# Feed-forward of an encoder: the first part's convolution, product and down projection moved behind the next parts' up projections

## The chip, the cores and the metric

The kernel runs on one core of a Trainium2 chip, in one launch. The metric is device microseconds of one execution. Five engines of the core work beside each other, each through its own queue in program order: TensorE (PE in the profile) for matrix products, VectorE (DVE), ScalarE (ACT), GpSimd (POOL) and SyncE (SP), which here issues the DMA transfers. An instruction that waits for a semaphore holds up what stands behind it in its own queue, and nothing else.

## The reference, cut to what matters

Two sequences (256 and 512 positions, 1024 wide) go through two layers. Each layer is a mixer (mLSTM, then windowed attention) and a feed-forward with a convolution of three taps along the sequence. The change touches the feed-forward alone:

```python
def conv_ffn(h, w_up, conv_w, conv_b, w_down):
    u = h @ w_up                                   # 1024 -> 2*2816
    u = conv_general_dilated(u, conv_w[:, None, :], padding=((1, 1),), ...) + conv_b
    g, val = u[..., :D_FF], u[..., D_FF:]
    return (silu(g) * val) @ w_down                # 2816 -> 1024
# in trunk, for each of DEPTH = 2 layers:
    x = x + g1 * y                                 # y: the mixer's output
    h = rmsnorm(x, norm_g[l, 1]) * (1 + sc2) + sh2
    x = x + g2 * conv_ffn(h, ...)
```

All of it is float32. A matrix product is made of three products of rounded halves (hi*hi, lo*hi, hi*lo), so each operand is split into a "hi" and a "lo" tile.

## The kernel before, in words

Both sequences lie side by side as 768 columns; channels lie on the 128 partitions. The hidden width 2816 is cut into 11 parts (NPART). A part has two units of up weights (i = 0 gives the gate rows, i = 1 the value rows, 256 channels each) and one unit of down weights. In the order of the code, a part p does this:

- **`up(p)`**: for i = 0 and 1 a `pair` makes the up product of 256 channels for all columns by a Strassen scheme: seven "quarters" (`quarters`, L1139 to L1146) of 12 matmuls each, 128 x 384. For part 0 a hand-ordered `head` does both units. For part 1 the head has done two of the seven quarters ahead ("rest"), so `pair` has five left. The quarters go by names in the code: `fifth()` fills the bank `e` from the weight sum `s1h`/`s1l`; T2 adds to the bank `b`, whose start is copied in by ACT (L1188); a copy of `b` into the bank `d` by ACT (L1199, the "fork") must stand before T3 adds to `d`; B22 finishes `b`; T4 finishes `d`, after ACT has copied `d` out at T3 (L1210). DVE joins `b` and `e` with these copies (L1212, L1213) into the row tile `urow`, and ACT writes the other halves (L1152).
- Each `pair` loads two weight tiles (`raw`, five buffers, SP), POOL makes sums and differences of them in place (L1172, L1175, L1176, L1184), and ACT and DVE split them: ACT casts the hi part (`whi`, `s1h`, L238), DVE subtracts for the lo part (`wlo`, `s1l`, L239).
- **`conv`**: per 128 channels one ACT instruction (L1357) and two on DVE (L1359, L1360), 128 x 772 each. A part has four such channel groups.
- **`silu`** (ACT, L1367) and **`product`**: POOL multiplies (L1372), ACT casts and DVE subtracts into the split tile `g`. silu of a part is handed to the next `pair`, which issues it behind its fork ("behind").
- **`down(p)`**: the down product, 16 tiles of 6 matmuls; DVE adds each tile to the residual (L567).

The order in which the code names the work is: up(p), then down(p-1), so a part's down product covers the time until the next part's pairs. The engines' queues are then set by a scheduler, which moves instructions within this order by its own estimate of times; `head` alone is fixed by hand. `urows` has one row tile for part 0 and one for all others.

For part 0 the convolution stands right behind the head, its gate and product are handed to the first pair of part 1, and down(0) comes behind the second pair of part 1.

Of the kernel before, what the change touches and what calls it, by code (L numbers as in the profile page):

```python
# [11 lines left out]
R = mybir.dt.float32r  # L12
# [3 lines left out]
P = 128  # L16
# [9 lines left out]
H = T // 2  # L26
# [3 lines left out]
TG = T + GAP  # L30
# [48 lines left out]
def col(t):  # L79

    return t + (GAP if t >= 256 else 0)
# [64 lines left out]
class Net:  # L146
# [1195 lines left out]
    def ffn(self, l, xt, pool, last_tile, apply, keep=None):  # L1342
        nc = self.nc
        u0 = U_FFN + l * NPART * 3
        early = self.prepare(u0)
        next(last_tile)

        urows = [self.slab([P, 4, TG]) for _ in range(2)]
        for urow in urows:
            nc.gpsimd.memset(urow[:, :, 256 : 256 + GAP], 0.0)  # L1350

        behind = []

        def conv(u, y, ch):
            cb = self.cst(CB + l * 44 + ch)
            w = lambda tap: self.cst(CW + (l * 44 + ch) * 3 + tap)
            nc.scalar.activation(y, u, AF.Identity, bias=cb, scale=w(1))  # L1357
            stt = nc.vector.scalar_tensor_tensor
            stt(y[:, 1:], u[:, :-1], w(0), y[:, 1:], ALU.mult, ALU.add)  # L1359
            stt(y[:, :-1], u[:, 1:], w(2), y[:, :-1], ALU.mult, ALU.add)  # L1360


        held = []

        def silu(yrow):
            for j in range(2):
                nc.scalar.activation(yrow[:, j], yrow[:, j], AF.Silu)  # L1367

        def product(yrow, g):
            for j in range(2):  # L1370
                y = yrow[:, 2 + j]
                nc.gpsimd.tensor_tensor(y, y, yrow[:, j], ALU.mult)  # L1372
                self.fp_copy_split(g[:, 0, j], g[:, 1, j], y)

        def up(p):
            urow = urows[0] if p == 0 else urows[1]
            fixed = lambda i: self.bank[i][:, :H]
            if p == 0:
                eng = mybir.EngineType
                self.ready(HALVES[0])  # L1380
                with self.tc.manual_schedule(engines={eng.PE, eng.Activation, eng.DVE}):
                    behind[:] = self.head(u0, last_tile, pool, urows, mark, early)
            yrow = self.slab([P, 4, TG])
            g = self.slab([P, 2, 2, TG], R)
            for i in range(2):
                if p:
                    rows = [urow[:, 2 * i + j] for j in range(2)]
                    with ExitStack() as order:
                        for ins in behind[2 * i :] if p == 1 else ():
                            order.enter_context(self.tc.issue_after(ins))  # L1390

                        other = p == i == 1
                        bank = lambda j: self.pa()[:, :H] if j == 1 and other else fixed(j)
                        self.pair(pool, u0 + 3 * p + i, bank, rows, p == 1, held.pop() if held else None)
                for j in range(2):
                    conv(urow[:, 2 * i + j], yrow[:, 2 * i + j], i * FC + 2 * p + j)
                if i == 0:
                    held.append(lambda: silu(yrow))
            if p:
                product(yrow, g)  # L1400
            else:
                gate = held.pop()
                held.append(lambda: (gate(), product(yrow, g)))
            return g

        def mark(t):

            hi, _ = self.quarter(self.B11)
            self.mm(t, hi[0][:, :P], hi[0], True, True)

        def down(p, g):
            ws = (w for _, w in self.halves(u0 + 3 * p + 2))
            chunk = lambda w, i: [t[:, 512 * i : 512 * (i + 1)] for t in w]

            def tile(w, c, rng):
                s0, s1, _ = rng
                o = self.pa()[:, : s1 - s0]
                cs = slice(c % 4 * P, (c % 4 + 1) * P)
                for i in range(2):
                    wh, wl = chunk(w, i)  # L1420
                    gh, gl = (g[:, z, i, col(s0) : col(s0) + s1 - s0] for z in range(2))
                    self.mm(o, wh[:, cs], gh, i == 0, False)
                    self.mm(o, wh[:, cs], gl, False, False)
                    self.mm(o, wl[:, cs], gh, False, i == 1)
                self.resid(xt, o, l, 40, c, rng)

            if p < NPART - 1:
                for h, w in enumerate(ws):
                    for rng in SAMPLE, PROMPT:
                        for c in range(4 * h, 4 * h + 4):  # L1430
                            tile(w, c, rng)
                return
            ws = list(ws)
            for rng in RANGES:
                norm = Norm(self, xt, rng, apply, last=keep is None and rng is RANGES[-1], adds=None if keep is not None else nc.vector)
                for c in range(KC):
                    tile(ws[c // 4], c, rng)
                    norm.square(c)
                    if keep is not None or rng is not RANGES[-1] or c < 3:
                        self.tick(0.65)  # L1440
                if keep is not None:
                    self.save_x(xt, keep, rng)
                self.start(rng, norm.stages())

        prev = None
        for p in range(NPART):
            g = up(p)
            if prev is not None:
                down(*prev)
            prev = (p, g)  # L1450
        down(*prev)


    def run(self):
# [182 lines left out]
```

## Time and profile before

| what | before |
|---|---|
| median of 3 runs | 1856.12 us (1850.48 to 1857.64) |
| the profiled execution | 1854.76 us, span 1852.7 us |
| PE busy | 1797.8 us, 97% of the span |
| DVE busy | 1394.0 us, 75% |
| ACT busy | 896.9 us, 48% |
| POOL busy | 482.4 us, 26% |
| granted PE clock, mean | 0.991 |

The feed-forward of layer 0 fills about 510 to 1045 us of the span, that of layer 1 about 1310 us to the end. The first parts stand at about 550 to 650 us and 1350 to 1450 us. In a timeline row stand the start, the duration, the engine, the line, the operation, the tiles written and read, the size, and in brackets the idle time of the engine before it and who ended it. In a windows row stand the stretch, its length, and for each engine its busy time and number of instructions.

### The profile page before, as it was taken

What the parts mean: (1) busy time and instruction counts of PE and PEld (TensorE: products, weight loads), DVE (VectorE), ACT (ScalarE), POOL (GpSimd) and SP (SyncE); (2) the same over time, 40 slices, a digit from 0 to 9 for tenths busy, and PEclk for the clock granted to TensorE, in tenths of its full rate; (3) what the DMA queues carried; (4) which work ended last, traced back from release to release, by engine and by line L of the source; (5) the groups of instructions that cost most, each with busy time, mean ns of one, the idle gap of its engine ahead of it and who ended that gap; (6) DMA issues with size and microseconds to landing.
All of it is one profiled execution on the core that took longest, in us unless ns stands there. A gap on an engine that the chain in (4) does not pass through costs nothing.

```text
span 1852.7 us, 29043 instructions
## 1 busy us (share of the span) xinstructions
PE 1797.8 (97%) x11270; PEld 1656.8 (89%) x11270; DVE 1394.0 (75%) x2296; ACT 896.9 (48%) x1816; POOL 482.4 (26%) x387
## 2 busy tenths in 40 slices
PE   7999999999999999999999999999999999999997
PEld 4987887888998999999999888889989999999996
DVE  4755676886689777777777768876898777777777
ACT  4444433444456444444444556764564444444443
POOL 1001001031024333333331303330134333333322
PEclk7999999999999999999999999999999999999999
DMA  8343556546312222222222321133122222222212
GB/s 330 116 148 131 171 192 222 164 143 206 102 46 78 71 67 67 68 69 70 66 69 87 103 83 50 48 95 117 58 83 77 69 69 69 69 69 69 69 35 69
DMA packets 64245, 184.48 MB, mean 100 GB/s; under 512 B 6167, under 2 KB 23831, under 8 KB 64108
## 3 DMA queue, kind: packets, MB, share of 16 engines
q1 hardware_dynamic: 64108, 182.63, 30.4%
q8 instruction: 88, 1.44, 0.3%
q14 instruction: 49, 0.40, 0.1%
HBM read 176.17 MB, written 6.43 MB: 99 GB/s over the span
## 4 chain that ended last, share of the span: by engine, by line
PE 84%; DVE 5%; issue 4%; DMA 3%; ACT 2%; POOL 1%; SPq 0%; POOLq 0%; ACTq 0%; DVEq 0%
PE ps L232 25%; PE pa L232 25%; PE ps L1139 10%; PE ps L1142 10%; PE ps L1140 10%; PE pa L978 1%; DMA raw<-in_adaln_w_dram 1%; DVE wlo L239 1%; DMA raw<-in_w_dram 1%; DVE slab L567 1%; DMA slab<-in_adaln_w_dram 0%; PE pa L1142 0%; PE pa L1140 0%; PE pa L1139 0%; ACT whi L238 0%
## 5 line engine op out<-in xcount | busy, mean ns | idle before, releaser
L238 ACT CAST whi<-raw 128x1024 fp32r<-128x1024 f32 x237 | 248.1, 1049 | 349.1 <-PE pa L232 162.3
L239 DVE TENSOR_TENSOR wlo<-raw,whi 128x1024 fp32r<-128x1024 f32 x237 | 319.6, 1349 | 112.8 <-ACT whi L238 110.9
L232 PE MATMUL pa<-slab,whi 128*128 128x256 f32 (+1 forms) x1472 | 347.4, 332 | 2.8 <-DVE slab L567 2.8
L232 PEld LDWEIGHTS pa<-slab,whi 128*128 128x128 f32 x1472 | 253.9, 189 | 27.1 <-DVE slab L567 4.1
L567 DVE SCALAR_TENSOR_TENSOR slab<-pa,mod,slab 128x256 f32<-128x256 f32 (+1 forms) x368 | 211.3, 592 | 72.0 <-PE pa L232 71.6
L232 PE MATMUL pa<-slab,wlo 128*128 128x256 f32 (+1 forms) x736 | 234.4, 330 | 0.0
L232 PE MATMUL ps<-zh,whi 128*128 128x256 f32 (+1 forms) x560 | 189.3, 339 | 3.7 <-ACT whi L238 1.7
L232 PE MATMUL ps<-zh,wlo 128*128 128x256 f32 (+1 forms) x560 | 184.1, 330 | 2.2 <-DVE wlo L239 2.2
L232 PE MATMUL ps<-zl,whi 128*128 128x256 f32 (+1 forms) x560 | 185.2, 332 | 0.7 <-DVE zl L530 0.7
L1139 PE MATMUL ps<-zh,whi 128*128 128x384 f32 x504 | 172.2, 342 | 3.7 <-ACT nt L1210 1.9
L1140 PE MATMUL ps<-zl,whi 128*128 128x384 f32 x504 | 169.9, 337 | 0.8 <-DVE zl L1096 0.8
L1142 PE MATMUL ps<-zh,wlo 128*128 128x384 f32 x504 | 168.9, 335 | 0.0
L232 PEld LDWEIGHTS pa<-slab,wlo 128*128 128x128 f32 x736 | 139.3, 189 | 13.1 <-DVE wlo L239 0.4
L1175 POOL TENSOR_TENSOR raw<-raw,raw 128x512 f32<-128x512 f32 x40 | 52.2, 1305 | 330.7 <-DVE wlo L239 246.3
L232 PE MATMUL ps<-slab,whi 128*128 128x384 f32 x512 | 132.2, 339 | 2.2 <-ACT sg L819 1.3
L1372 POOL TENSOR_TENSOR slab<-slab 128x772 f32<-128x772 f32 x44 | 86.5, 1968 | 167.6 <-DVE slab L1360 155.7
L1359 DVE SCALAR_TENSOR_TENSOR slab<-slab,cstt,slab 128x771 f32<-128x771 f32 x88 | 104.7, 1192 | 26.6 <-ACT slab L1357 26.4
L232 PEld LDWEIGHTS ps<-zh,whi 128*128 128x128 f32 x560 | 107.4, 192 | 17.5 <-issue 4.4
L484 DVE SCALAR_TENSOR_TENSOR ada<-raw,silc,ada 128x1024 f32<-128x1024 f32 x84 | 110.2, 1349 | 15.1 <-DMA raw<-in_adaln_w_dram 14.9
L232 PEld LDWEIGHTS ps<-zl,whi 128*128 128x128 f32 x560 | 107.4, 192 | 13.0 <-issue 3.4
L232 PEld LDWEIGHTS ps<-zh,wlo 128*128 128x128 f32 x560 | 107.3, 192 | 12.5 <-DVE wlo L239 3.1
L1172 POOL TENSOR_TENSOR raw<-raw 128x512 f32<-128x512 f32 x40 | 64.3, 1608 | 200.2 <-DMA raw<-in_w_dram 161.3
(292 smaller groups left out, 4294.3 us busy)
## 6 DMA issues: line engine op xcount, KB each, us to landing
raw<-in_w_dram SPq DMA_DIRECT2D x208, 512.0 KB, 3.8
raw<-in_adaln_w_dram SPq DMA_DIRECT2D x84, 512.0 KB, 4.6
slab<-in_x_dram SPq DMA_DIRECT2D x12, 512.0 KB, 7.0
slab<-in_adaln_w_dram SPq DMA_DIRECT2D x12, 512.0 KB, 10.3
slab<-mrows SPq DMA_DIRECT2D x8, 384.0 KB, 5.7
xs<-slab SPq DMA_DIRECT2D x6, 512.0 KB, 3.9
bt<-brow SPq DMA_DIRECT2D x16, 192.0 KB, 3.0
slab<-xs SPq DMA_DIRECT2D x6, 512.0 KB, 6.4
```

The lines of the kernel that those rows point to most:

```text
L232: self.nc.tensor.matmul(out, lhsT, rhs, start=start, stop=stop)
L238: nc.scalar.copy(hi, src)
L239: return nc.vector.tensor_tensor(lo, src, hi.bitcast(F32), ALU.subtract)
L484: stt(acc[:, s], row, w, acc[:, s], ALU.mult, ALU.add)
L567: self.nc.vector.scalar_tensor_tensor(x, o, self.mod[l][:, gc + c, q : q + 1], x, ALU.mult, ALU.add)
L1139: mm(o, wh[:, k], hi[k], start=start and k == 0, stop=False, skip_group_check=True)
L1140: mm(o, wh[:, k], lo[k], start=False, stop=False, skip_group_check=True)
L1142: mm(o, wl[:, k], hi[k], start=False, stop=k == 3, skip_group_check=True)
L1172: tt(q[2], q[2], q[3], ALU.add)
L1175: tt(q[0], q[2], q[0], ALU.subtract)
L1359: stt(y[:, 1:], u[:, :-1], w(0), y[:, 1:], ALU.mult, ALU.add)
L1372: nc.gpsimd.tensor_tensor(y, y, yrow[:, j], ALU.mult)
```

## The change

For part 0, `up` now returns after the head. Its convolution, gate and product are issued by the new function `gated` behind the second pair of part 1 (with their own tiles `yrow` and `g`, taken later), ahead of the convolution of that second pair's rows. down(0) moves behind the two pairs of part 2 and stands right ahead of part 2's product and down(1). From part 3 on the order is as before. No instruction is added or taken away on any engine.

```diff
         def up(p):
...
-            yrow = self.slab([P, 4, TG])
-            g = self.slab([P, 2, 2, TG], R)
+            if p == 0:
+                return
             for i in range(2):
...
+                    self.pair(pool, u0 + 3 * p + i, bank, rows, p == 1, held.pop() if held else None)
+                if p == i == 1:
+
+                    gs.append(product(gated(urows[0], 0, (0, 1))))
+                if i == 0:
+                    yrow = self.slab([P, 4, TG])
+                gated(urow, p, (i,), yrow)
+            return yrow
+
+        def gated(urow, p, sides, yrow=None):
+            yrow = self.slab([P, 4, TG]) if yrow is None else yrow
+            for i in sides:
                 for j in range(2):
                     conv(urow[:, 2 * i + j], yrow[:, 2 * i + j], i * FC + 2 * p + j)
-                if i == 0:
+                if i == 0 and p:
                     held.append(lambda: silu(yrow))
-            if p:
-                product(yrow, g)
-            else:
-                gate = held.pop()
-                held.append(lambda: (gate(), product(yrow, g)))
-            return g
+                elif i == 0:
+                    silu(yrow)
+            return yrow
...
+        gs = []
         for p in range(NPART):
-            g = up(p)
-            if prev is not None:
-                down(*prev)
-            prev = (p, g)
-        down(*prev)
+            yrow = up(p)
+            if p == 2:
+
+                down(0, gs[0])
+            if p:
+                gs.append(product(yrow))
+            if p > 1:
+                down(p - 1, gs[p - 1])
+        down(p, gs[p])
```

What the scheduler makes of it stands in the queues. Behind the second T2 quarter of part 1 (it reads `whi_772` before and `whi_769` after, and writes bank `ps_640`), PE's queue before holds the whole fifth quarter of part 2's first pair and then down(0):

```order
L1142 MATMUL ps_640_4535<-zh_94,wlo_773_5696 128x384
L1139 MATMUL ps_639_4534<-zh_94,s1h_807_5941 128x384
L1140 MATMUL ps_639_4534<-zl_95,s1h_807_5941 128x384
L1142 MATMUL ps_639_4534<-zh_94,s1l_808_5942 128x384
L1139 MATMUL ps_639_4534<-zh_94,s1h_807_5941 128x384
```

After, at the same place:

```order
L1142 MATMUL ps_640_4535<-zh_94,wlo_770_5673 128x384
L1139 MATMUL ps_639_4534<-zh_94,s1h_783_5799 128x384
L1140 MATMUL ps_639_4534<-zl_95,s1h_783_5799 128x384
L1139 MATMUL ps_638_4533<-yh_4540,whi_781_5793 128x384
L1140 MATMUL ps_638_4533<-yl_4541,whi_781_5793 128x384
L1139 MATMUL ps_641_4536<-zh_94,whi_771_5676 128x384
```

So only four matmuls of part 2 stand between T2 and T3 (bank `ps_641`, the second pair of part 1), where before there were a quarter and 12 matmuls of down(0).

ACT's queue from the start copy of that pair's bank `b` (L1188) to its fork (L1199), before:

```order
L1188 COPY ps_640_4535<-slab_713_5137 128x384
L238 CAST s1h_807_5941<-raw_803_5930 128x512
L1193 COPY nt_777_5705<-pa_776_5703 128x384
L1357 ACTIVATE slab_756_5577<-slab_713_5137,cstt_75 128x772
L238 CAST whi_780_5790<-raw_779_5788 128x1024
L1152 COPY slab_713_5137<-ps_641_4536 128x128
L1152 COPY slab_713_5137<-ps_641_4536 128x256
L238 CAST slab_755_5564<-slab_754_5563 128x772
L1357 ACTIVATE slab_756_5577<-slab_713_5137,cstt_75 128x772
L1199 COPY ps_641_4536<-ps_640_4535 128x384
```

and after (`slab_712` holds part 0's rows, `slab_713` part 1's, `slab_776` part 0's `yrow`, `slab_764` part 1's):

```order
L1357 ACTIVATE slab_764_5653<-slab_713_5137,cstt_75 128x772
L1188 COPY ps_640_4535<-slab_713_5137 128x384
L1357 ACTIVATE slab_776_5753<-slab_712_5136,cstt_75 128x772 x4
L238 CAST s1h_783_5799<-raw_779_5788 128x512
L1193 COPY nt_774_5682<-pa_773_5680 128x384
L238 CAST whi_781_5793<-raw_780_5790 128x1024
L1152 COPY slab_713_5137<-ps_641_4536 128x128
L1152 COPY slab_713_5137<-ps_641_4536 128x256
L1367 ACT_TABLE_LOAD
L1367 ACTIVATE slab_776_5753<-slab_776_5753 128x772
L1357 ACTIVATE slab_764_5653<-slab_713_5137,cstt_75 128x772
L1199 COPY ps_641_4536<-ps_640_4535 128x384
```

All four convolution instructions of part 0, the table load and a silu now stand ahead of the fork.

POOL's queue at the same place, before:

```order
L1184 TENSOR_TENSOR raw_768_5683<-raw_768_5683,raw_769_5685 128x512
L1172 TENSOR_TENSOR raw_803_5930<-raw_803_5930 128x512
L1372 TENSOR_TENSOR slab_754_5563<-slab_754_5563 128x772
L1172 TENSOR_TENSOR raw_815_6056<-raw_815_6056 128x512
L1175 TENSOR_TENSOR raw_804_5932<-raw_803_5930,raw_804_5932 128x512
```

and after:

```order
L1184 TENSOR_TENSOR raw_765_5660<-raw_765_5660,raw_766_5662 128x512
L1373 TENSOR_TENSOR slab_776_5753<-slab_776_5753 128x772
L1175 TENSOR_TENSOR raw_780_5790<-raw_779_5788,raw_780_5790 128x512
L1373 TENSOR_TENSOR slab_776_5753<-slab_776_5753 128x772
L1176 TENSOR_TENSOR raw_780_5790<-raw_780_5790 128x512
L1184 TENSOR_TENSOR raw_779_5788<-raw_779_5788,raw_780_5790 128x512
```

The two products of part 0 (L1373, the former L1372) now alternate with the weight sums of part 2's first pair (`raw_779`, `raw_780`). In SP's queue the two loads of down(0)'s weights stand behind the four loads of part 2's pairs instead of ahead of them. From part 4 on all queues are the same in both kernels, but for numbers.

More of the change, by code (lines that the diff above doesn't have):

```diff
@@ L1367, in silu, with product @@
                 nc.scalar.activation(yrow[:, j], yrow[:, j], AF.Silu)
-        def product(yrow, g):
+        def product(yrow):
+            g = self.slab([P, 2, 2, TG], R)
             for j in range(2):
@@ L1373, in product @@
                 self.fp_copy_split(g[:, 0, j], g[:, 1, j], y)
+            return g
         def up(p):
@@ L1382, in up @@
                     behind[:] = self.head(u0, last_tile, pool, urows, mark, early)
-            yrow = self.slab([P, 4, TG])
-            g = self.slab([P, 2, 2, TG], R)
+            if p == 0:
+                return
             for i in range(2):
-                if p:
[L1387 to L1394, printed above, removed]
+                rows = [urow[:, 2 * i + j] for j in range(2)]
+                with ExitStack() as order:
+                    for ins in behind[2 * i :] if p == 1 else ():
+                        order.enter_context(self.tc.issue_after(ins))
+                    other = p == i == 1
+                    bank = lambda j: self.pa()[:, :H] if j == 1 and other else fixed(j)
+                    self.pair(pool, u0 + 3 * p + i, bank, rows, p == 1, held.pop() if held else None)
[8 more added lines that the diff above has]
+            for i in sides:
                 for j in range(2):
                     conv(urow[:, 2 * i + j], yrow[:, 2 * i + j], i * FC + 2 * p + j)
-                if i == 0:
+                if i == 0 and p:
                     held.append(lambda: silu(yrow))
-            if p:
-                product(yrow, g)
-            else:
-                gate = held.pop()
-                held.append(lambda: (gate(), product(yrow, g)))
-            return g
+                elif i == 0:
+                    silu(yrow)
+            return yrow
         def mark(t):
@@ L1443, in down @@
                 self.start(rng, norm.stages())
-        prev = None
+        gs = []
         for p in range(NPART):
-            g = up(p)
-            if prev is not None:
-                down(*prev)
-            prev = (p, g)
-        down(*prev)
+            yrow = up(p)
[6 more added lines that the diff above has]
+        down(p, gs[p])
     def run(self):
```

## The prediction

> **What bounds the kernel now.** I read the page first: busy times, then the chain that ended last.
>
> ```profile
> span 1852.7 us, 29043 instructions
> PE 1797.8 (97%) x11270; PEld 1656.8 (89%) x11270; DVE 1394.0 (75%) x2296; ACT 896.9 (48%) x1816; POOL 482.4 (26%) x387
> PE 84%; DVE 5%; issue 4%; DMA 3%; ACT 2%; POOL 1%; SPq 0%; POOLq 0%; ACTq 0%; DVEq 0%
> ```
>
> PE carries the end. So I asked the windows where PE is not full inside the feed-forwards: the middle parts, and the first parts of layer 0 and of layer 1.
>
> ```profile
> 700.00:1000.00 300.00, 300.00 (x1706) 285.16 (x1706) 227.75 (x256) 142.11 (x225) 104.81 (x63) 1.00 0.23 71
> 560.00:580.00 20.00, 17.01 (x91) 15.48 (x90) 19.96 (x17) 13.94 (x22) 10.43 (x5) 1.00 0.26 82
> 1360.00:1380.00 20.00, 16.98 (x91) 15.38 (x90) 19.96 (x17) 13.95 (x22) 10.25 (x5) 1.00 0.27 82
> ```
>
> The middle parts have no idle PE at all, and there the queues of both kernels agree. At the first parts PE idles 3.0 us per layer while DVE (third pair of numbers) is full: 19.96 of 20. Both layers look alike, so I work out one and double it. The waits there, by the view of waits for 555 to 580 us, and how PE's rows start around them:
>
> ```profile
> PE ps L1142 <- DVE s1l L239: 1.4, 1, 1.4
> PE ps L1139 <- ACT nt L1210: 0.9, 1, 0.9
> PE ps L1139 <- ACT ps L1188: 0.7, 1, 0.7
> ...
> 567.22 0.34 PE L1142 MATMUL pa<-zh,s1l 128*128 128x384 f32 x1
> 568.49 0.44 PE L1139 MATMUL ps<-zh,whi 128*128 128x384 f32 x1 [0.93 <-ACT nt L1210]
> ...
> 570.17 0.33 PE L1139 MATMUL ps<-zh,whi 128*128 128x384 f32 x1
> 570.52 0.34 PE L1142 MATMUL ps<-zh,wlo 128*128 128x384 f32 x1
> 571.55 0.44 PE L1139 MATMUL ps<-zh,whi 128*128 128x384 f32 x1 [0.70 <-ACT ps L1188]
> ...
> 573.94 0.34 PE L1140 MATMUL ps<-zl,s1h 128*128 128x384 f32 x1
> 575.64 0.45 PE L1142 MATMUL ps<-zh,s1l 128*128 128x384 f32 x1 [1.36 <-DVE s1l L239]
> ```
>
> Undisturbed, matmuls start 0.174 us apart (570.17 to 570.52 is two). The three waits cost start to start 1.27, 1.03 and 1.70 less 0.174 each, with some 0.1 us lost in the restart rows counted in neither: 3.5 us, and I take **3.8 us** with these restarts. That is all the change can win here.
>
> **The change, part by part.** No instruction is added or removed; all is order. Four moves have one answer together: down(0)'s 96 matmuls and 16 residual adds, its two weight loads on SP, part 0's eight convolution instructions on DVE and four on ACT, and its product. As work they cost the same later. The loads are hidden: DMA's share at this place is 0.26 (the last column but one in the windows). What counts is what they covered. Before, down(0) gave PE work while DVE, ACT and POOL made part 2's weights. After, PE runs the pairs of parts 1 and 2 without it, while part 0's convolution still stands in the same stretch.
>
> I count time from t = 0, the end of the B22 quarter of part 1's first pair, since the first convolution of part 1 waits for it. First PE's side, by its queue after: 10 matmuls of the fifth quarter, 12 of T4, 12 of T2 and the four of part 2, then T3 of the second pair: 38 x 0.174 = 6.6 us.
>
> *The fork (L1199) behind ACT's queue.* The lengths, as starts of neighbours that did not wait:
>
> ```profile
> 558.40 1.05 ACT L1357 ACTIVATE slab<-slab,cstt 128x772 f32<-128x772 f32 x1
> 559.34 0.50 ACT L1199 COPY ps<-ps 128x384 f32<-128x384 f32 x1
> 559.85 1.28 ACT L1367 ACT_TABLE_LOAD   x1
> 561.15 0.85 ACT L1367 ACTIVATE slab<-slab 128x772 f32<-128x772 f32 x1
> 561.90 1.04 ACT L238 CAST whi<-raw 128x1024 fp32r<-128x1024 f32 x1
> 562.84 0.53 ACT L1152 COPY slab<-pa 128x128 f32<-128x128 f32 x2
> ...
> 571.02 0.48 ACT L1188 COPY ps<-slab 128x384 f32<-128x384 f32 x1 [2.58 <-DVE slab L1212]
> 571.44 0.62 ACT L238 CAST s1h<-raw 128x512 fp32r<-128x512 f32 x1
> 571.96 0.47 ACT L1193 COPY nt<-pa 128x384 f32<-128x384 f32 x1
> ```
>
> So: convolution 0.94, fork 0.50, table load 1.30, silu 0.75, cast of a weight tile 0.94, two copies out 0.45, start copy 0.42, small cast 0.52, copy of e 0.42. In the queue after, ahead of the fork: a weight cast that waits for a buffer which B22 reads (done at 1.15), then convolution, start copy, four convolutions, small cast, copy of e, cast, copies out, table load, silu, convolution: 0.94 + 0.42 + 3.76 + 0.52 + 0.42 + 0.94 + 0.45 + 1.30 + 0.75 + 0.94 = 10.4. The fork ends at 1.15 + 10.4 + 0.5 = 12.1, PE came at 6.6: a new wait of **5.5 us**. Behind it on PE stands everything of part 2. Two small casts of part 2 that PE meets on the way are inside this time. The first pair's own fork has only three matmuls (0.52) of cover for its 0.50 and the run-out of T2 (0.34): **0.4 us**.
>
> On the table load the Trainium skill (ScalarE: Activation LUTs, "What ACT_TABLE_LOAD costs") says that a switch costs 1.28 us and another 1.38 us of drain. Here the load takes the same 1.28, but the silu starts 0.02 us after it and the load 0.01 us after the fork, so no drain shows. By that page of the Trainium skill the wait would be 6.9 us and the sum some 2.8 us higher over both layers.
>
> *The next start copy (L1188, part 2's first pair) behind DVE.* DVE's lengths, and what POOL does to them:
>
> ```profile
> 560.11 1.21 DVE L239 TENSOR_TENSOR wlo<-raw,whi 128x1024 fp32r<-128x1024 f32 x1
> 561.25 0.68 DVE L239 TENSOR_TENSOR s1l<-raw,s1h 128x512 fp32r<-128x512 f32 x1
> 561.85 1.01 DVE L1359 SCALAR_TENSOR_TENSOR slab<-slab,cstt,slab 128x771 f32<-128x771 f32 x1
> 562.89 2.51 DVE L1360 SCALAR_TENSOR_TENSOR slab<-slab,cstt,slab 128x771 f32<-128x771 f32 x1
> 565.32 2.31 DVE L239 TENSOR_TENSOR wlo<-raw,whi 128x1024 fp32r<-128x1024 f32 x1
> ...
> 578.67 1.01 DVE L1360 SCALAR_TENSOR_TENSOR slab<-slab,cstt,slab 128x771 f32<-128x771 f32 x1
> 579.61 0.95 DVE L239 TENSOR_TENSOR slab<-slab,slab 128x772 fp32r<-128x772 f32 x1
> 580.48 1.01 DVE L1359 SCALAR_TENSOR_TENSOR slab<-slab,cstt,slab 128x771 f32<-128x771 f32 x1
> ...
> 584.37 0.56 DVE L1213 TENSOR_TENSOR slab<-pa,nt 128x384 f32<-128x384 f32 x1 [1.34 <-ACT nt L1210]
> 584.84 0.55 DVE L1212 TENSOR_TENSOR slab<-ps,nt 128x384 f32<-128x384 f32 x1
> ```
>
> ```profile
> 562.08 2.51 POOL L1372 TENSOR_TENSOR slab<-slab 128x772 f32<-128x772 f32 x1 [5.97 <-ACT slab L1367]
> 564.54 2.01 POOL L1184 TENSOR_TENSOR raw<-raw,raw 128x512 f32<-128x512 f32 x1
> 573.19 1.84 POOL L1372 TENSOR_TENSOR slab<-slab 128x772 f32<-128x772 f32 x1 [4.43 <-DVE slab L1360]
> 590.69 1.29 POOL L1175 TENSOR_TENSOR raw<-raw,raw 128x512 f32<-128x512 f32 x1 [13.02 <-issue]
> ```
>
> Beside POOL, instructions on both sides stretch: L1360 2.51 instead of 1.01, a weight lo 2.31 instead of 1.21, a product 2.51 instead of 1.84. How much of POOL's time lands on DVE, I take from the stretch in which DVE never waits:
>
> ```profile
> 553.15:582.90 29.75, 26.76 (x146) 25.14 (x145) 29.71 (x27) 20.28 (x33) 12.62 (x6) 1.00 0.32 105
> ```
>
> Its DVE instructions, at 1.14 (weight lo), 0.60 (s1l), 0.94 (convolution), 0.87 (product lo), 0.47 (joins), are 5, 4, 12, 2 and 3: 22.5 us. POOL's six, undisturbed, 4 x 1.29 + 2 x 1.84 = 8.8. So 7.2 us of 8.8, or 0.8, land on DVE.
>
> After, DVE's queue from the first weight lo behind t = 1.2 to the join L1212 of part 1's second pair holds 12 convolutions, 2 weight lo, 1 s1l, 2 product lo and 2 joins: 16.8 us. POOL stands beside it with two products and three weight sums: 7.5 us, of which 6.0. So the join ends at 24.0; behind it ACT does convolution, cast, copies and start copy (2.9): T2 of part 2's first pair can start at 26.9. PE comes with 94 matmuls (16.3) and the 5.5: 21.8. Second wait **5.1 us**, between 0 (POOL takes nothing) and 6.6 (all of 7.5).
>
> For the upper end there is a rule: the Trainium skill (SBUF — State Buffer, "SBUF: two separate sides") calls the port pair of VectorE and GpSimd an exclusive lock held for a whole instruction. The stretched rows agree; by it, with nothing hidden, the sum would be 3 us higher over both layers.
>
> *T2 of part 2's second pair*: the same queues go on with 12.5 us of DVE and 6.0 from POOL, to 42.5; PE, 84 matmuls and two of slack behind 26.9, comes at 41.8: **0.7 us** (0 to 2.3). Then down(0) and down(1) follow each other, 33 us of PE, in which DVE catches up; at nothing, by the stretch 700 to 1000 us above, in which six down products run and PE never idles.
>
> Sum per layer: 0.4 + 5.5 + 5.1 + 0.7 - 3.8 = 7.9; both layers 15.8. The profiled execution took 1854.8 (2.1 around its span; 1.4 under the median of 1856.1), so 1870.6; I say **1871 us**.
>
> **The rivals.** (1) *The convolution fits after all.* The three waits go, no others come: 1854.8 - 7.6 = 1847. For it: POOL's weight sums and DVE's order are what held PE before, and both are relieved for part 1. Against: ACT's queue to the fork needs 10.4 us whatever DVE does. It decides for itself where ACT reaches the fork by 6.6. (2) *Only the fork waits*: POOL costs DVE little, since its work falls into DVE's idle time; 2 x (5.9 - 3.8) = 4 more, 1859, no change that shows. Against: the products start only when the convolution ends, so POOL runs where DVE is fullest. (3) *down(0) and down(1) in a row stall too*, as four `pa` banks wait for DVE adds between weight lo tiles of part 3; two weight lo and a blocked one (1.14 + 2.31) late per down, some 3 us per layer: 1877.
>
> **How the numbers follow.** My forecast 0.60 (1864 to 1875), rival 2 0.22, rival 1 0.08, rival 3 0.10. About 0.5%, 9.3 us, is what a measurement of this kernel can tell from no change: slower means above 1865.4, faster below 1846.8. Rival 2 and nearly all of rival 1 lie within; faster is left with 0.03, since 7.6 us is under the bound; same 0.27, slower 0.70. The range runs from rival 2's low side to all upper ends (0.4 + 5.5 + 6.6 + 2.3 - 3.8 = 11.0, twice, 1877) and rival 3: 1857 to 1880.
>
> **What would show it.** Right: the old waits (1.4, 0.9, 0.7) are gone; about 5 us of PE wait for ACT L1199 once per layer, behind the four L1357 and the table load; a wait for ACT L1188 or for a lo tile some 10 us of PE work later; no idle in the middle parts; 560:600 with some 10 us less PE busy than its length. Wrong: L1199 in time (then ACT's order on the chip lets it through sooner), or DVE rows beside POOL unstretched, or idle in the two down products.

## The result: slower by 1%, 1872 us

The changed kernel takes 1872.24 us (median of 5 runs, 1870.58 to 1874.99), the kernel before 1855.68 us (median of 5). The ratio is 1.0096, with a 95% interval of 1.0082 to 1.011: slower by 16 us. The prediction said 1871, within 1857 to 1880.

The page of the changed kernel first: the span, and busy time by engine.

```profile
span 1873.0 us, 29085 instructions
PE 1806.5 (96%) x11270; PEld 1663.9 (89%) x11270; DVE 1397.5 (75%) x2296; ACT 897.5 (48%) x1816; POOL 480.2 (26%) x387
```

DVE, ACT and POOL do what they did before, within 4 us; the 42 instructions that the span line has more than before are waits for semaphores. PE has 9 us more busy time with the same 11270 matmuls, which is the first sign of something that the prediction left out: matmuls that take longer. Outside the two first parts, matmul starts lie as far apart as before, to 1.6 us at any place and to about 1 us in all. The new time stands in 540 to 700 us and 1340 to 1500 us. The profiled run is the slowest of the five (1874.99 us), so its trace shows some 20 us of new time where the medians show 16.6.

PE's waits there, layer 0 of the changed kernel (us in total, how many, the longest):

```profile
PE ps L1139 <- ACT ps L1188: 3.5, 1, 3.5
PE ps L1139 <- ACT ps L1199: 3.3, 1, 3.3
PE ps L1139 <- ACT whi L238: 0.7, 1, 0.7
PE ps L1139 <- ACT s1h L238: 0.7, 1, 0.7
```

The old three (s1l 1.4, L1210 0.9, L1188 0.7) are gone. In their place stand the fork L1199, with two small casts of part 2 just ahead of it, and the start copy L1188 of part 2's first pair. Layer 1 looks alike (3.3 and 2.4). This is ACT's queue up to the fork, in the timeline of the changed kernel:

```profile
566.20 1.05 ACT L238 CAST whi<-raw 128x1024 fp32r<-128x1024 f32 x1 [1.52 <-PE ps L1140]
567.15 1.03 ACT L1357 ACTIVATE slab<-slab,cstt 128x772 f32<-128x772 f32 x1
568.09 0.47 ACT L1188 COPY ps<-slab 128x384 f32<-128x384 f32 x1
568.50 3.81 ACT L1357 ACTIVATE slab<-slab,cstt 128x772 f32<-128x772 f32 x4
...
574.57 1.28 ACT L1367 ACT_TABLE_LOAD   x1
575.87 0.85 ACT L1367 ACTIVATE slab<-slab 128x772 f32<-128x772 f32 x1
576.62 1.02 ACT L1357 ACTIVATE slab<-slab,cstt 128x772 f32<-128x772 f32 x1
577.54 0.47 ACT L1199 COPY ps<-ps 128x384 f32<-128x384 f32 x1
...
592.54 0.49 ACT L1188 COPY ps<-ps 128x384 f32<-128x384 f32 x1
```

t = 0 of the prediction, the end of the quarter that releases the first of these rows, is 566.1 here. The fork ends at 578.0, 11.9 behind it (12.1 was forecast); the start copy ends at 593.0, 26.9 behind it (26.9 was forecast). So both walks through the queues held. What PE does behind each wait shows the part that was not foreseen (timeline of PE; not every matmul is shown):

```profile
578.06 0.69 PE L1139 MATMUL ps<-zh,whi 128*128 128x384 f32 x1 [3.26 <-ACT ps L1199]
...
579.19 0.52 PE L1139 MATMUL ps<-zh,whi 128*128 128x384 f32 x1
...
580.15 0.52 PE L1139 MATMUL ps<-zh,whi 128*128 128x384 f32 x1
...
581.78 0.34 PE L1139 MATMUL ps<-bq,whi 128*128 128x384 f32 x1
...
593.08 0.69 PE L1139 MATMUL ps<-zh,whi 128*128 128x384 f32 x1 [3.46 <-ACT ps L1188]
...
597.09 0.52 PE L1139 MATMUL ps<-yh,whi 128*128 128x384 f32 x1
```

From 579.19 to 580.15 there are three matmuls: 0.32 us each instead of 0.174. The quarter from 578.06 to 581.78 takes 3.72 us instead of 2.09. The windows of the changed kernel give the granted clock (third figure from the end):

```profile
572.00:578.00 6.00, 1.44 (x6) 0.60 (x4) 6.00 (x8) 5.97 (x11) 0.20 (x1) 1.00 0.00 1
578.00:589.00 11.00, 10.94 (x54) 10.94 (x55) 11.00 (x7) 4.72 (x8) 10.93 (x5) 0.84 0.00 1
589.00:593.00 4.00, 0.62 (x4) 0.30 (x2) 3.96 (x5) 3.40 (x7) 0.00 (x0) 0.83 0.10 14
593.00:597.00 4.00, 3.92 (x12) 3.92 (x13) 4.00 (x4) 2.62 (x5) 2.66 (x1) 0.50 0.71 217
597.00:600.00 3.00, 3.00 (x14) 3.00 (x14) 2.45 (x4) 0.70 (x3) 1.28 (x1) 0.75 0.12 46
```

Behind each wait of over 3 us PE runs at half its clock for a while. The Trainium skill (TensorE: Matmul & The Clock Gate, "What's actually happening") says that the clock falls to half after at least one idle window of about 3.4 us, and is whole again after a busy one of about 3.4 us. The trace agrees on the half and on the way back (0.50 behind both waits, 1.00 again 3 to 7 us later). It shows that less idle time is enough: around the second wait the clock falls at 591.7 us, 2.0 us after the last matmul and while PE still waits, which is why the row from 589 us has 0.83. In the kernel before, whose longest wait here is 1.4 us, the granted clock in this place is 1.00.

### The profile page after: what moved, and what is told of

The parts are those of the page before. It is cut to its first block, busy times and chain, and to the rows that moved or that the text cites. A ratio compares the mean times of both kernels' runs of the same rounds, so it can differ in the third digit from the quotient of the medians.

```text
span 1873.0 us, 29085 instructions
## 1 busy us (share of the span) xinstructions
PE 1806.5 (96%) x11270; PEld 1663.9 (89%) x11270; DVE 1397.5 (75%) x2296; ACT 897.5 (48%) x1816; POOL 480.2 (26%) x387
## 4 chain that ended last, share of the span: by engine, by line
PE 83%; DVE 7%; DMA 4%; ACT 3%; issue 2%; POOL 1%; SPq 0%; POOLq 0%; ACTq 0%; DVEq 0%
PE ps L232 26%; PE pa L232 24%; PE ps L1139 10%; PE ps L1140 10%; PE ps L1142 10%; DMA raw<-in_adaln_w_dram 1%; PE pa L978 1%; DVE wlo L239 1%; DMA slab<-in_adaln_w_dram 1%; DVE slab L567 1%; DVE slab L1360 1%; ACT whi L238 1%; DMA raw<-in_w_dram 1%; DVE slab L239 1%; PE pa L1139 1%
## 5 line engine op out<-in xcount | busy, mean ns | idle before, releaser
L567 DVE SCALAR_TENSOR_TENSOR slab<-pa,mod,slab 128x256 f32<-128x256 f32 (+1 forms) x368 | 212.4, 593 | 77.5 <-PE pa L232 77.1
L1373 POOL TENSOR_TENSOR slab<-slab 128x772 f32<-128x772 f32 x44 | 87.7, 1992 | 189.7 <-DVE slab L1360 163.6
L232 PEld LDWEIGHTS ps<-zh,whi 128*128 128x128 f32 x560 | 107.0, 191 | 17.2 <-issue 4.4
L1139 PEld LDWEIGHTS ps<-zh,whi 128*128 128x128 f32 x504 | 96.4, 191 | 21.2 <-ACT ps L1199 10.7
```

The costliest lines, as they stand in the source:

```text
L232: self.nc.tensor.matmul(out, lhsT, rhs, start=start, stop=stop)
L567: self.nc.vector.scalar_tensor_tensor(x, o, self.mod[l][:, gc + c, q : q + 1], x, ALU.mult, ALU.add)
L1139: mm(o, wh[:, k], hi[k], start=start and k == 0, stop=False, skip_group_check=True)
```

## The experiments

The first question was which of the two moves costs the time, and whether ACT's queue, DVE, or the half clock is what holds PE. All ratios are against the kernel before, with 95% intervals.

**1. Only down(0) late.** The order of before, with one move:

```diff
             g = up(p)
-            if prev is not None:
+            if p == 2:
+                down(*first)
+            if prev is not None and p != 1:
                 down(*prev)
+            if p == 0:
+                first = (p, g)
             prev = (p, g)
```

> The kernel before with one edit: down(0) comes behind part 2's pairs, ahead of down(1); the convolution, gate and product of part 0 stay right behind the head, as before. Theory A (the new waits come from part 0's convolution and product standing in the stretch where ACT and DVE are full, not from down(0) itself): the three old waits stay, the fork L1199 of part 1's second pair is in time, and DVE, which was free of part 0's work at 583 us before, joins part 1's second pair in time for the next start copy: 1851 to 1859 us. Rival B (what costs is that PE lost down(0) as cover between the pairs): nearly all of the 16 us is here too, 1866 to 1873 us, with a wait for L1188 or a lo tile at part 2's first pair.

Measured: 1868.48 us, 1.0076 (1.0063 to 1.0088). Theory A fell; rival B holds. The waits of PE, layer 0:

```profile
PE ps L1139 <- ACT nt L1210: 4.8, 2, 2.6
PE ps L1142 <- DVE s1l L239: 1.4, 1, 1.4
PE ps L1142 <- DVE wlo L239: 1.3, 1, 1.3
PE ps L1139 <- ACT ps L1188: 0.7, 2, 0.4
```

The fork is in time, as I had said, but L1210 and a lo tile are late instead. My error was to read "DVE is free at 583" from a trace in which down(0)'s 16.7 us of PE work follow there. Without them PE asks for part 2's tiles at once.

**2. Only the convolution and product late.** The changed kernel with `if p == 1` in place of `if p == 2` ahead of `down(0, gs[0])`.

> The changed kernel with one edit: down(0) comes right behind part 1's second pair again, as before; the convolution, gate and product of part 0 stay behind part 1's second pair. Theory A: the fork's wait for ACT stays (5.4 us per layer by the trace of the changed kernel) and the half clock after it; the second wait turns into one of PE for the product of part 0 on DVE, some 3 us: per layer -3.8 + 0.4 + 5.5 + 2 + 3, about 7, so 1866 us, 1860 to 1872. Rival B (down(0) is the cover that matters): with down(0) back, little is lost, 1852 to 1859 us.

Measured: 1869.42 us, 1.0075 (1.0061 to 1.0088), as theory A had it. The wait for L1199 is 5.3 us, and down(0) then waits 1.9 us (`pa`, L567). So each move alone costs some 14 us, and both together 17. They are not two costs that add up, but two ways to overdraw the same stretch.

**3. The fork ahead of part 0's ACT work.**

```diff
-                    gs.append(product(gated(urows[0], 0, (0, 1))))
+                    with self.tc.issue_after(self.fork_ins):
+                        gs.append(product(gated(urows[0], 0, (0, 1))))
```

> The changed kernel with one edit: the ACT instructions of part 0's convolution, gate and product are held behind the fork L1199 of part 1's second pair. Theory A: the fork stands at 6.3 us from t = 0 instead of 12.1, so the wait for L1199 goes and so does the half clock after it. On DVE ten convolution instructions instead of twelve stand ahead of the join of part 1's second pair, and only weight sums of POOL beside them: join at 18, so no wait for L1188 at part 2's first pair, and the rest of DVE's work falls before part 2's second pair, where some 4 us of wait appear (DVE at 41, PE at 37). Per layer -3.8 + 0.4 + 4: 1856 us, 1851 to 1864. Rival C (DVE and POOL are the bound of the whole stretch, ACT's order only decides where PE waits): the same 10 us come later, 1868 to 1873.

Measured: 1872.57 us, 1.0099 (1.0085 to 1.0113): no gain at all. PE's waits, layer 0:

```profile
PE ps L1139 <- ACT ps L1188: 4.9, 2, 3.0
PE ps L1142 <- DVE wlo L239: 1.5, 1, 1.5
PE ps L1139 <- ACT nt L1211: 1.1, 1, 1.1
```

The 5.4 us at the fork are gone (it ends at 572.5, and PE does not wait for it), and nearly the same time comes back at the next four waits (L1188 twice). This is rival C. The intervals of this run and of the changed kernel overlap, so a gain of two or three us could hide in them; one of 5 us per layer could not.

**4. Work for PE inside the waits.** Behind T2 of part 1's second pair, and ahead of T2 of part 2's first:

```diff
+            with self.tc.issue_after(self.last.ins):
+                for k in range(16):
+                    self.mm(t, hi[0][:, :P], hi[0], k == 0, k == 15)
```

> The changed kernel with 16 further matmuls of 128x384 (2.8 us) per place, whose result nobody reads, behind T2 of part 1's second pair and ahead of T2 of part 2's first pair, where PE waits for L1199 and L1188. Theory D (the waits of over 3 us make the granted clock fall to half for 3.4 to 6.8 us, and that is a loss of its own, some 4 us per layer): the added matmuls lie inside the waits, the clock stays at 1.00, PE comes earlier to the second wait, and what is left is the half-rate time behind the second wait, 2 to 2.5 us per layer: 1867 us, 1864 to 1870. Rival E (the half clock is only in the records, or hidden by the next wait): 1871 to 1878 us, as what is not hidden of the added 2 x 2.8 us per layer is added.

Measured: 1872.06 us, 1.0093 (1.008 to 1.0107). The time is rival E's, at its lower end, but the clock did as theory D said (windows of this kernel, to set beside those of the changed one):

```profile
572.00:578.00 6.00, 6.00 (x36) 6.00 (x36) 6.00 (x7) 5.94 (x10) 0.66 (x1) 1.00 0.00 1
578.00:589.00 11.00, 11.00 (x64) 10.75 (x62) 11.00 (x9) 5.88 (x9) 10.05 (x5) 1.00 0.01 2
593.00:597.00 4.00, 1.19 (x7) 0.87 (x5) 3.97 (x3) 0.95 (x3) 3.15 (x1) 1.00 0.47 135
```

It is 1.00 to 597 us, PE is full to 589 us, and 11.1 us of added matmuls (64 x 0.174) over both layers cost no time. But nothing is won either: PE now waits 3.3 us at the next fork instead (593 to 597; the forks have the line L1203 here):

```profile
PE ps L1139 <- ACT ps L1203: 3.7, 2, 3.3
```

So the half clock behind the first two waits is not what costs the 16 us: it mostly fills time in which PE would wait anyway. That it costs nothing at all is not shown. Behind the last wait the clock falls here too (for 3.4 us from 598.4), and by matmul starts this kernel's first parts, the added matmuls included, are 1.3 and 1.8 us shorter in the two layers than in the trace of the changed one, while the medians (1872.06 and 1872.24) show no gain. In all three rows DVE (third pair) is full. So the next theory was that DVE's work is the bound.

**5. Without DVE's taps for part 0.**

```diff
+            if ch % FC < 2:
+                return
             stt = nc.vector.scalar_tensor_tensor
```

> The changed kernel, with the eight tap instructions (L1359, L1360) of part 0's convolution on DVE left out in each layer; all else stays, ACT's four L1357 and its table load too. Theory F (new, from the four runs before: DVE is full from 567 to 601 us and its total work there is the bound; which engine's order holds PE only decides where PE waits): 7.5 us of DVE per layer fall out, and with them nearly all of the new waits, 7 to 9.7 us per layer: 1856 us, 1852 to 1859. Rival G (ACT's queue ahead of the fork is a cost of its own): the wait for L1199 stays at 5 us with its half clock, the one for L1188 goes: 1865 us, 1862 to 1868.

Measured: 1867.75 us, 1.0068 (1.0052 to 1.0085). Theory F in this plain form fell, and G's number was met without G's mechanism. 15 us of DVE work over both layers were taken away and 5 us came back. PE's waits, layer 0:

```profile
PE ps L1142 <- DVE wlo L239: 2.6, 2, 1.4
PE ps L1139 <- ACT ps L1188: 1.6, 1, 1.6
```

The two waits of 0.7 us for ACT's casts stay as well. The products now come sooner and POOL's work falls in one piece on a DVE that prepares part 2: the lo tile takes 2.02 us instead of 1.21, the tap behind it 2.43 instead of 1.01 (timeline of DVE):

```profile
575.43 2.02 DVE L239 TENSOR_TENSOR wlo<-raw,whi 128x1024 fp32r<-128x1024 f32 x1 [2.78 <-ACT whi L238]
577.54 2.43 DVE L1361 SCALAR_TENSOR_TENSOR slab<-slab,cstt,slab 128x771 f32<-128x771 f32 x1
```

DVE is no longer full here: it idles 2.78 us ahead of this lo tile, and 2.34 us a little earlier, until ACT's casts come, and these stand behind part 0's four L1357 in ACT's queue, the later one behind a table load and a silu too.

**6. POOL's work of parts 0 to 2 on DVE, in the changed kernel.** `nc.vector` in place of `nc.gpsimd` for the sums in `pair` and for `product`, while p < 3.

> The changed kernel, with POOL's weight sums (L1172 to L1184) and products of parts 0 to 2 given to DVE. In the stretch 567 to 601 us of the changed kernel POOL has 15 us of work, about 7 sums and 3 products. Theory F with the price of the prediction (0.8 of POOL's time lands on DVE): DVE is rid of 11.6 us and gets 7 sums at 0.6 and 3 products at 0.87, 6.8 us, so 4.8 us per layer are won: 1862 us, 1858 to 1866. Rival H (POOL's work costs DVE nothing): DVE has 6.8 us per layer more, 1886 us, 1880 to 1890.

Measured: 1868.74 us, 1.0067 (1.0055 to 1.008). Rival H is refuted: DVE has more to do in this stretch and still holds PE up less, by 2.7 us per layer. How that can be stands in the groups of instructions on DVE, 567 to 601 us. The changed kernel (count, busy us, mean ns):

```profile
L1360 DVE SCALAR_TENSOR_TENSOR slab<-slab,cstt,slab 128x771 f32<-128x771 f32 x8 | 10.8, 1345 | 0.1
L1359 DVE SCALAR_TENSOR_TENSOR slab<-slab,cstt,slab 128x771 f32<-128x771 f32 x8 | 10.6, 1344 | 0.0
L239 DVE TENSOR_TENSOR slab<-slab,slab 128x772 fp32r<-128x772 f32 x3 | 5.2, 1720 | 0.0
```

With POOL's work on DVE (567 to 600 us):

```profile
L1360 DVE SCALAR_TENSOR_TENSOR slab<-slab,cstt,slab 128x771 f32<-128x771 f32 x8 | 8.2, 1019 | 0.0
L1359 DVE SCALAR_TENSOR_TENSOR slab<-slab,cstt,slab 128x771 f32<-128x771 f32 x8 | 8.0, 1021 | 0.3 <-ACT slab L1357 0.2
L1373 DVE TENSOR_TENSOR slab<-slab 128x772 f32<-128x772 f32 x4 | 3.8, 956 | 0.0
L239 DVE TENSOR_TENSOR slab<-slab,slab 128x772 fp32r<-128x772 f32 x3 | 2.9, 960 | 0.0
```

The same 19 instructions take 26.6 us beside POOL and 19.1 without it: 7.5 us of stretch, for four products and three sums that POOL does in 11.2 us when alone (4 x 1.84 + 3 x 1.29). That is 0.67 of POOL's time; the prediction had taken 0.8. The Trainium skill (SBUF — State Buffer, "SBUF: two separate sides") has a lock on a shared port pair, held for a whole instruction, and these rows agree with it for the taps and the splits. On DVE itself the seven cost 3.8 + 3 x 0.69 = 5.9, so 1.6 us per layer would be won by this price, an estimate from these rows; 2.7 were measured, and the rest is not accounted for. (In the second window DVE does six sums, since the next pair's three come sooner.) The expected gain of 4.8 us per layer was too large because it took POOL's stretched 15 us, and seven sums instead of three, as its undisturbed work.

**7. The same edit in the kernel before.**

> The kernel before with the same edit: POOL's weight sums and products of parts 0 to 2 are given to DVE. In its full stretch, 553 to 583 us, POOL has four sums and two products, 8.8 us. Theory F: DVE is rid of 7.0 us and gets 4.1, so 2.9 of the 3.8 us of old waits per layer go: 1849 us, 1846 to 1853; this would be faster than both kernels. Rival H: 4.1 us per layer more on a full DVE, 1863 us, 1859 to 1867.

Measured: 1859.83 us, 1.0019 (1.001 to 1.0029). Theory F's 1849 was missed. The reason is another place:

```profile
PE ps L1140 <- DVE zl L1096: 1.9, 2, 1.7
PE ps L1139 <- ACT nt L1210: 1.8, 1, 1.8
```

Part 1's first sums now stand in DVE's queue ahead of the tiles of the input (L1096), for which PE waits at once.

**8 and 9. Without any of part 0's row work, after and before.** In `up`, `gated` and `product` are not called for part 0 (in the kernel before: `for j in range(2) if p else ()`), and down(0) reads the tiles `zh` and `zl`.

> The changed kernel with all of part 0's row work left out in each layer: convolution, gate, product (ACT, DVE and POOL); down(0) multiplies the layer's input tiles instead of the product. Theory I (part 0's row work, put into this stretch, is too much for ACT, DVE and POOL together; the late down(0) is harmless in itself): no PE wait of over 1 us is left at the pairs of parts 1 and 2, the old three waits are gone too: 1850 us, 1846 to 1854. Rival J (without down(0) between them the pairs of parts 1 and 2 alone starve PE, whatever part 0 does): 3 to 6 us of waits per layer stay, 1856 to 1864 us.

> The kernel before with the same work left out: part 0's convolution, gate and product in each layer; down(0) multiplies the layer's input tiles. The control to the run above. Both theories: the three old waits (3.8 us per layer) go, 1847 us, 1843 to 1851. By theory I it equals the changed kernel without part 0's row work within 0.3%; by rival J it is 9 us or more under it.

Measured: the changed kernel without it 1858.22 us, 1.0017 (1.0008 to 1.0027); the kernel before without it 1847.06 us, 0.9964 (0.9952 to 0.9975). They are 11 us apart, so rival J holds: down(0) out of its place costs that much even when part 0's rows ask nothing of ACT, DVE and POOL. Of over 0.5 us there are two waits left in the first (layer 0) and none in the second:

```profile
PE ps L1142 <- DVE wlo L239: 1.3, 1, 1.3
PE pa L232 <- DVE slab L567: 0.9, 1, 0.9
```

The second of them is PE in down(0) and down(1), waiting for the residual adds. In the window that holds most of down(0) DVE is full, where the prediction had it catch up:

```profile
605.00:630.00 25.00, 24.01 (x134) 21.07 (x133) 24.54 (x29) 9.78 (x17) 7.11 (x4) 1.00 0.28 85
```

By matmul starts, the two kernels are 4.3 and 4.6 us apart here in the two layers, which is 9 of the 11 us; the two waits are half of it, and several of under 0.5 us the rest.

**10. The products of parts 0 and 1 alone on DVE, in the kernel before.**

```diff
-                nc.gpsimd.tensor_tensor(y, y, yrow[:, j], ALU.mult)
+                (nc.vector if self.on_dve else nc.gpsimd).tensor_tensor(y, y, yrow[:, j], ALU.mult)
```

> The kernel before, with the products (L1372) of parts 0 and 1 given to DVE, and POOL's weight sums left on POOL. In the run that moved the sums too, those of part 1's first pair came ahead of the input tiles on DVE (a new wait of 1.4 to 1.9 us for L1096); here they don't. If POOL's product is what stretches DVE ahead of the old waits (2.51 instead of 1.01, 2.31 instead of 1.21), 1 to 1.5 us per layer are won: 1852 us, 1849 to 1855. If not, DVE has 1.7 us per layer more: 1858 us.

Measured: 1850.55 us, 0.9977 (0.9968 to 0.9986): faster than both kernels. Of the three old waits one is left (layer 0):

```profile
PE ps L1139 <- ACT ps L1188: 1.1, 1, 1.1
```

The time is in the expected range, and the rows of DVE in the two kernels show where it comes from: ahead of the join of part 1's second pair, s1l takes 0.68 us instead of 2.14, a weight lo 1.21 instead of 2.32, a product lo 0.95 instead of 2.03. DVE is at the end of that join (L1212) 29.4 us behind the start of the first s1l instead of 32.2, of which 1.3 were idle, although it does two products more. Where POOL's weight sums still run, the rows stay long (2.05 for a tap, 2.32 for a weight lo).

**11. Experiments 3 and 6 together.**

> The changed kernel with two edits at once: part 0's ACT instructions held behind the fork L1199, and POOL's sums and products of parts 0 to 2 on DVE. Each alone left 1872.6 and 1868.7 us. Theory I (ACT's order, DVE and POOL hold PE in turn, so reliefs of two add up to more than their sum): the 3.3 us for L1199 that are left with POOL's work on DVE go, 1861 us, 1857 to 1864. Rival C (a fixed amount of work of DVE is the bound, ACT's order only decides where PE waits): as with POOL's work on DVE alone, 1866 to 1871 us.

Measured: 1866.92 us, 1.0063 (1.0049 to 1.0077): as with POOL's work on DVE alone. Rival C. The wait for the fork went, and one of 4.4 us for L1188 came.

**12. Without ACT's part of part 0.** The changed kernel without the four L1357 and two silus of part 0; the first tap reads the row tile.

> The changed kernel, with ACT's part of part 0's convolution and gate left out in each layer: the four L1357 and the two silus (5.3 us of ACT; the table load stays, for part 1's silu). The first tap starts from the row tile itself, so DVE's eight taps and POOL's two products stay. It completes the set: without DVE's part 1867.8, without all three engines' parts 1858.2. Rival G (ACT's queue ahead of the fork is what costs): the 5.4 us wait per layer and its half clock go, 1862 us, 1858 to 1865. Rival C (DVE is held by its own work and POOL's, ACT's order decides only where PE waits): the wait moves to L1188, a lo tile or a join: 1871 us, 1868 to 1874.

Measured: 1872.09 us, 1.0088 (1.0075 to 1.0102). Rival C again: 5.3 us of ACT per layer, most of them ahead of the fork, taken away, win nothing that the medians show. The wait stands at the next copy, behind DVE's join:

```profile
PE ps L1139 <- ACT ps L1188: 5.7, 2, 5.1
PE pa L232 <- DVE slab L567: 0.8, 1, 0.8
```

Together: in the changed kernel, relief of ACT alone wins nothing clear of the intervals (3, 12), nor does filling PE (4); relief of DVE from the taps or from POOL wins some 5 us each (5, 6), and relief of all three wins 14 (8). The stretch from part 1's first join to part 2's last is held first by DVE and by what POOL does to it. With DVE's taps gone, POOL's share and ACT's queue hold PE next. How the rest of experiment 5's relief divides between these two was not tested.

## Why the prediction was right, and where it was not

- *The old waits, -3.8 per layer*: right, all three are gone. Experiment 9, in which they go and no others come, is 3.2 and 3.4 us shorter here by matmul starts, so 3.8 was a little too much.
- *First pair's fork, 0.4*: 0.24 start to start.
- *The fork L1199, 5.5*: at its place it is right. The two casts (0.82 and 0.87 start to start), the wait (3.43) and the slow first row behind it (0.31) make 5.4. The table load takes 1.28 us, and the silu starts 0.02 us behind it, so again no drain shows. The 2.8 us that the prediction would add to the sum for a drain do not follow from its own walk either: a fork later by 1.38 us makes the second wait shorter by as much.
- *The start copy L1188, 5.1*: its end was forecast to 0.1 us; the wait was 3.5 and 2.4 in the two layers. The step that failed is PE's side, "PE comes with 94 matmuls (16.3) and the 5.5". It takes every matmul at 0.174 us, but the quarter behind the first wait ran at half clock and took 1.6 us longer (the slow first row is in it).
- *T2 of part 2's second pair, 0.7*: no wait. The half clock behind the second wait (quarters of 4.01 and 2.74 us instead of 2.09 each) had already taken 2.6 us there.
- *down(0) and down(1) in a row, 0*: 0.2 us in layer 0, 0.6 in layer 1 for L567. Small here, but the cover named for it ("DVE catches up") is weak: in experiment 8 DVE is full in that window.
- *The sum, 7.9 per layer*: by matmul starts 9.8 and 10.5 in the profiled run, the slowest of the five. The two terms for half clock that were missing, some 4 us per layer, are partly offset by the smaller second wait and the missing third. The medians are 16.6 us apart, the forecast was 15.8. That they agree to 1 us is in part luck, since these errors nearly cancel.

The sum also holds for another reason than the one given. Its terms read as separate costs with an owner each: ACT's queue 5.5, DVE 5.1. They are not. The prediction's own walk has DVE's join end at 24.0 and the start copy at 26.9 whatever happens at the fork, while PE alone would be there at 16.3; these 10.6 us are one debt of DVE, and the 5.5 lie inside it. That fits with what was seen when the fork's wait was taken away (3, 12) or filled (4): PE waited at later places, and the time hardly changed. The debt has two sources, and how much each owes depends on which is moved first. down(0) gone from between the pairs costs 11 to 14 us by itself (experiments 8 against 9, and 1), and part 0's row work placed later then adds some 3 to 4 (the changed kernel against 1). But the row work moved alone, with down(0) in its place, costs 14 us as well (2).

Of the rivals, *the convolution fits* and *only the fork waits* fell with the waits shown. *Down(0) and down(1) in a row stall too* is real, but under 1 us per layer.

## What to carry to other kernels

When several engines stand behind one bound, don't sell the waits one by one: walk the engine that is full (here DVE with its share of POOL) from the last point where it was free to the last point where PE needs it, and take that one difference. A block of PE work that asks little of the others, like down(0), is worth something as cover at the place where they are full, and moving it costs that cover even if the work it covered moves too: here 5.5 to 7 us per layer of down(0)'s 16.7 (8 against 9, and 1). Where two engines slow each other, a product that DVE does itself (0.96 us) can cost DVE less than one that POOL does beside it (0.67 of 1.84 us, 1.2 us, by the estimate of experiment 6); moving four of them gave the one version with all of the work that beats both kernels (0.9977).

## What was not expected of the hardware

PE's granted clock fell to half around waits of 3.26 and 3.46 us, and matmuls then started 0.32 us apart instead of 0.174, for the length of one to two quarters. It fell with the 5.1 us wait of experiment 12 too (0.83 over 580 to 600 us), and stayed at 1.00 where the same waits were filled with matmuls (experiment 4, to 598 us). But one long wait is not needed. In experiment 5 two short ones were enough (timeline of PE, not every matmul is shown):

```profile
575.46 0.44 PE L1139 MATMUL ps<-yh,whi 128*128 128x384 f32 x1 [0.72 <-ACT whi L238]
...
577.50 0.44 PE L1142 MATMUL ps<-yh,wlo 128*128 128x384 f32 x1 [1.43 <-DVE wlo L239]
...
578.40 0.53 PE L1139 MATMUL ps<-yh,whi 128*128 128x384 f32 x1
578.72 0.53 PE L1140 MATMUL ps<-yl,whi 128*128 128x384 f32 x1
```

In experiment 1 a wait of 2.56 us left the clock at 1.00 in layer 0, and one of the same 2.56 us was followed by 0.50 in layer 1 (1393.6 to 1397.0 us). The clock records of the 14 traces show a pattern. In each trace the stretches at half start a whole number of times 3.41 us apart, and in the first parts they last 3.41 or 6.83 us. When the time is cut into slots on this grid, then in the first parts all 19 slots at full clock in which PE idled 1.99 us or more were followed by one at half, and none was in which it idled 1.54 us or less; between 1.6 and 1.9 us both occur. (The ends of matmuls are modelled, so the idle times are not exact.) So two equal waits can end differently, by how they lie to the slots. What the half clock costs of its own in this kernel was not separated (experiment 4).
